# A Mamba-2 and attention trunk on one core: three steps of the gated norm moved one step ahead, a token half in a tile of its own, low parts set off the 256-byte line

## The chip, the cores and the metric

One core of one Trainium2 chip. The metric is the device time of one execution in microseconds, the median of three runs. The profile is that of one execution, taken by the hardware profiler. PE is the matrix engine (PEld its weight loads), DVE the vector engine, ACT the scalar engine, POOL the one that also issues some DMAs, SP the one whose queue issues most of them.

## What is computed

256 tokens of width 2048 run through a Mamba-2 layer, a gated MLP with a short convolution, an attention layer (one block of 256 keys, so plain causal attention with a distance penalty) and a second MLP. After each of the four, the stream is normalised:

```
mix = mamba2_mixer(h, ...)                    # layer 0
h = layer_norm(ALPHA * h + mix, g, b)
h = layer_norm(ALPHA * h + conv_ffn(h, ...), g, b)
k_blk, v_blk, k_mean = shared_kv(h, w_kv)
mix = moba_cross_attention(h, ...)            # layer 1
h = layer_norm(ALPHA * h + mix, g, b)
h = layer_norm(ALPHA * h + conv_ffn(h, ...), g, b)
```

The end of the Mamba-2 mixer, which the change touches, is for each of 8 groups of 512 channels

```
y = y * silu(z)
yg = y * rsqrt(mean(square(y)) + eps) * norm_w
```

All inputs are float32.

## The kernel before

**High and low parts.** Every float32 operand of a large product is split into a high part (rounded to fp32r) and a low part (the rest), and a product is made of three: high by high, low by high, high by low. A weight step is 512 KB: `load` fetches it into `raw` through SP's queue, `split` (L184, L185) has ACT write the high part `hi` and DVE the low part `lo`, each [128, 2, 512]. Four of each are held, and `splits` runs up to four steps ahead of the products. Activations live in `hT`, `yT`, `aT`, `gT`, with high and low part side by side.

**Chunks and steps.** The weights are cut into chunks of 512 output columns, the chunks into 882 steps of one weight tile each, all in one list worked off in order by the loop at the end. There are three modes:

- W (`whole`, L244 and L246): the weights are stationary, the activations move. A step has eight 512-wide matmuls on high parts (high and low activations beside each other) and eight 256-wide ones on low parts. Odd steps take the low parts first, so that runs of sixteen of a kind stand end to end. 560 steps are of this mode.
- X (`half`, L207, L208, L212): the activations are stationary, the weights move, 512 columns wide, once for each half of the 256 tokens, six matmuls a half.
- H: the dt chunk, with the same code as W.

All tiles in SBUF that TensorE reads in these modes start at one residue modulo 512 bytes, as their sizes are whole multiples of it (`LINE` pads small ones to 256 bytes).

**What runs beside the products.** `at(i, f)` puts a function behind the products of step i; `amid`, `within` and `beyond` put it inside a step. The instructions go to each engine in the order in which they are written, and every engine works off its own queue in order. For group g of the Mamba layer, with s0 the first step of its x chunk, the z chunk starts at s0 + 8 and the next group's x chunk at s0 + 16. `y_off` and `y_diag` (PE, then DVE) stand at s0 + 18; then `z_gate` (DVE, L768) at s0 + 20, `z_square` (ACT, L771) at s0 + 21, `z_sum` (two DVE additions, L775 and L776) at s0 + 22, `z_rms` (PE, L781, with the matrix of means) at s0 + 23, and five more steps to s0 + 28. The convolution of the next group has its taps on ACT (L575) and DVE (L580) behind step s0 + 21, and the decays on ACT (`m_decay`, L691) behind s0 + 21 and s0 + 22. POOL issues the loads of `mA` and `eA` (L668, L697) behind s0 + 19.

**The four sums and their norms.** `chain` works on the four X chunks of an output projection (`chs`, 2048 columns). As a chunk ends, `add2` or `add` (L393 to L406) adds ALPHA times the residual `r`, which `fetch` has loaded, and takes statistics. Chunk 3 is worked in another order, to have half 0 of the tokens normalised while half 1 is still summed: it has a `tail` of 4 steps (8 in the last of the four sums, `LAST`), in which only half 0 is done step by step, and half 1 of these steps comes at the end, in two pieces of 256 columns. In the kernel before, half 1 of this chunk is summed in the two pieces of 256 columns (`ch.piece`) in all its steps, tail or not: `second` calls `half` twice. The pieces lie in two of the three `acc` pairs of PSUM, in the last sum in the two `tp` tiles. `turn_half` (L349 on PE, L353 on ACT, L354 on DVE) turns normalised tokens back into `hT`, through `tp` tiles. The last sum keeps gains and shifts in free `acc` pairs (`gb_psum`, L454).

Of the kernel before, what the change touches and what calls it, by code (L numbers as in the profile page):

```python
# [19 lines left out]
F32R = mybir.dt.float32r  # L20
AF = mybir.ActivationFunctionType
OP = mybir.AluOpType
AX = mybir.AxisListType

P = 128
D = 2048
S = 256
# [9 lines left out]
ALPHA = 4.0 ** 0.25  # L37
LN_EPS = 1e-5
RMS_EPS = 1e-5
NC = 512  # L40
HC = NC // 2
NEG = -1.0e30
LINE = 64
# [10 lines left out]
WARM0 = 18  # L54
HEAD, TAIL = 3, 4
LAST = 8
SPARE = 3


# [32 lines left out]
def yoco_kernel(ctx: ExitStack, tc: tile.TileContext, x, lmg, lmb, lfg, lfb, x_t, columns, w, out):  # L92
    nc = tc.nc
    base = ctx.enter_context(tc.tile_pool(name="base", bufs=1))
    wts = ctx.enter_context(tc.tile_pool(name="wts", bufs=LA + 1))
# [8 lines left out]
    def acc_pair():  # L104
        return psum.tile([P, 2, NC], F32, tag="acc", name="acc", bufs=3)

    def tp_tile():
        return psum.tile([P, NC], F32, tag="tp", name="tp", bufs=2)
# [16 lines left out]
    steps, plan = [], chunks()  # L125
# [47 lines left out]
    def split():  # L173
        i = pos["split"]
        pos["split"] += 1
        t = raw_t.pop(i)
        if i in spare:
            h, l = (bufs["h"][:, k:k + 2].rearrange("p k a t -> p k (a t)") for k in (spare[i], spare[i] + 2))
        else:
            h = wts.tile([P, 2, NC], F32R, tag="hi", name="hi")  # L180
            l = wts.tile([P, 2, NC], F32R, tag="lo", name="lo")
        for e in ((0,), (1,)) if i < 2 else ((0, 1),):
            sl = slice(e[0], e[-1] + 1)
            nc.scalar.copy(h[:, sl], t[:, sl])  # L184
            nc.vector.tensor_sub(l[:, sl], t[:, sl], h[:, sl].bitcast(F32))  # L185
        hi_t[i], lo_t[i] = h, l
        load()
# [9 lines left out]
    def half(i, t, piece=None):  # L197

        ch, s = steps[i]
        h, l = hi_t[i], lo_t[i]  # L200
        sl = slice(0, NC) if piece is None else slice(piece * HC, (piece + 1) * HC)
        a = ch.part[t] if piece is None else ch.piece[piece]
        ts = slice(t * P, (t + 1) * P)
        for kk in range(2):
            k = 2 * s + kk
            th = ch.x.hi(k)[:, ts]
            nc.tensor.matmul(a, th, h[:, kk, sl], start=k == 0, stop=False)  # L207
            nc.tensor.matmul(a, th, l[:, kk, sl], start=False, stop=False)  # L208
        run(inner, (i, t, piece))
        for kk in range(2):  # L210
            k = 2 * s + kk
            nc.tensor.matmul(a, ch.x.lo(k)[:, ts], h[:, kk, sl], start=False, stop=k == ch.nk - 1)  # L212
        run(outer, (i, t, piece))

    def second(i):

        if steps[i][0].tail:
            half(i, 1, 0)
            half(i, 1, 1)
        else:  # L220
            half(i, 1)

    def done(i):
        hi_t.pop(i), lo_t.pop(i)
# [1 line left out]
    def whole(i):  # L226
        ch, s = steps[i]
        h, l = hi_t[i], lo_t[i]
        nj = ch.nj
        h, l = (t.rearrange("p a (k n) -> p (a k) n", n=nj * P) for t in (h, l))  # L230
        k0, half = ch.place(s)
        banks = [p[:, j, :] for p in ch.part[half:] for j in range(2)]

        parts = (1, 0) if s % 2 and ch not in calm else (0, 1)
        order = [(p, kk, j) for p in parts for kk in range(ch.per) for j in range(nj)]
        for n, (p, kk, j) in enumerate(order):
            if n == len(order) * 3 // 8:
                run(mid, i)
                splits(i)
            k = k0 + kk  # L240
            begins, ends = k == 0 and p == parts[0], k == ch.nk - 1 and p == parts[1]
            js = slice(j * P, (j + 1) * P)
            if p == 0:
                nc.tensor.matmul(banks[j], h[:, kk, js], ch.x.both(k), start=begins, stop=ends, skip_group_check=True)  # L244
            else:
                nc.tensor.matmul(banks[j][:, :S], l[:, kk, js], ch.x.hi(k), start=begins, stop=ends,  # L246
                                 skip_group_check=True)

    def products(i):
        ch, s = steps[i]  # L250
        if ch.mode == "W":
            if s == 0:
                ch.part = []
            if s == 0 or (not ch.both and s == ch.n // 2):
                ch.part += [acc_pair() for _ in range(1 + ch.both)]
        elif s == 0:
            a = acc_pair()
            ch.part = [a[:, 0, :], a[:, 1, :]] if ch.mode == "X" else [a]
            if ch.tail:
                ch.part.pop()  # L260
                ch.piece = [tp_tile()[:, :HC] if ch.tail == LAST else acc_pair()[:, 0, :HC] for _ in range(2)]
        if ch.mode != "X":
            whole(i)
            return done(i)
        half(i, 0)
        if i >= ch.end - ch.tail:
            if i < ch.last:
                return splits(i)
            for q in range(2):
                for j in range(ch.end - ch.tail, ch.end):  # L270
                    half(j, 1, q)
                    if q:
                        done(j)
        elif s < ch.head - 1:
            if ch.tail:
                splits(i)
        elif s == ch.head - 1:
            for j in range(ch.first, i + 1):
                if j < i or ch.tail:
                    splits(i, 1)  # L280
                second(j)
                done(j)
            if not ch.tail:
                splits(i, 1)
        else:
            run(mid, i)
            splits(i)
            second(i)
            done(i)
# [3 lines left out]
    def run(d, i):  # L293
        for f, a in d.get(i, []):
            f(*a)

    def at(i, f, *a):
        post.setdefault(i, []).append((f, a))
# [4 lines left out]
    def amid(i, f, *a):  # L303
        mid.setdefault(i, []).append((f, a))
# [5 lines left out]
    def beyond(i, t, q, f, *a):  # L310

        outer.setdefault((i, t, q), []).append((f, a))
# [52 lines left out]
    class Norm:  # L365
# [24 lines left out]
        def add(self, c, h, q=None):  # L390
            r = self.r[c][:, h]
            if q is None:
                nc.vector.scalar_tensor_tensor(r, r, ALPHA, self.chs[c].part[h], op0=OP.mult, op1=OP.add)  # L393
            else:
                v = r[:, q * HC:(q + 1) * HC]
                nc.vector.scalar_tensor_tensor(v, v, ALPHA, self.chs[c].piece[q], op0=OP.mult, op1=OP.add)
            for w in (0, 1) if q is None else (q,):
                nc.vector.bn_stats(self.st[:, h, 2 * c + w, :], r[:, w * HC:(w + 1) * HC])

        def add2(self, c):  # L400
            for h in range(2):
# [87 lines left out]
    chA = summed("a")  # L489
    up1, down1 = ffn_chunks(LAST)  # L490
    n_steps = len(steps)
# [325 lines left out]
    for g in range(NG):  # L817
        s0 = chX[g].first
        at(s0 + 3, m_load, g)
        at(s0 + 3, m_into, g)  # L820
        at(s0 + 7, m_cb, g)
        at(s0 + 9, m_bc, g)
        at(s0 + 5, m_decay, g, 0)
        at(s0 + 6, m_decay, g, 1)
        at(s0 + 9, m_exp, g, 0)
        at(s0 + 10, m_exp, g, 1)
        at(s0 + 10, m_into_exp, g)
        conv4(chX[g], 4 * g, lambda g=g: x_new(g), 0).plan()
        at(s0 + 11, x_silu, g)
        at(s0 + 11, m_mask, g, 0)  # L830
        at(s0 + 12, m_mask, g, 1)
        at(s0 + 13, x_turn, g)
        at(s0 + 13, y_d, g)
        for b in range(2):
            at(chZ[g].ready(b), z_gather, g, b)
            at(chZ[g].ready(b) + 1, z_silu, g, b)
        at(s0 + 18, y_off, g)
        at(s0 + 18, y_diag, g)
        at(s0 + 20, z_gate, g)
        at(s0 + 21, z_square, g)  # L840
        at(s0 + 22, z_sum, g)
        at(s0 + 23, z_rms, g)
        at(s0 + 24, z_log, g)
        at(s0 + 25, z_root, g)
        at(s0 + 26, z_newton, g)
        at(s0 + 27, z_scale, g)
        at(s0 + 28, z_split, g)


    def chain(norm, nxt=None, after=None):  # L850

        chs = norm.chs
        last = chs[3].last
        at(chs[0].first, norm.open)
        for c in range(4):
            at(max(chs[0].first, chs[c].last - 7), norm.fetch, c)
            if c < 3:
                at(chs[2].first + 3 + c, norm.fetch_gb, c)
                amid(chs[c].end, norm.add2, c) if c < 2 else beyond(chs[2].end, 0, None, norm.add2, c)
        beyond(last, 0, None, norm.add, 3, 0)  # L860
        beyond(last, 0, None, norm.stats, 0)
        if not nxt:
# [5 lines left out]
        n = nxt.first  # L868
# [49 lines left out]
    n3 = Norm(down1, keep(2), lfg[1], lfb[1], gb_last, lambda c: tok_view(out[0], c))  # L918
# [142 lines left out]
    for h in range(HEADS):  # L1061
        i, j = divmod(h, 4)
# [16 lines left out]
    end = n_steps - 1  # L1079
    chain(n3)  # L1080
    for e in range(4):
        spare[end - 3 + e] = 4 * e
    for c in (0, 2):
        at(down1[3].first + 6, n3.gb_psum, c)
    at(end - 6, n3.fetch_gb, 3)

    def rest(h):
# [62 lines left out]
```

## Time and profile before

| | |
|---|---|
| median of three runs | 2557.95 us (2557.05 to 2558.04) |
| span of the profiled execution, first to last instruction | 2555.2 us |
| granted TensorE clock, mean | 0.999 |
| HBM read | 492.30 MB, 196 GB/s |

The time of the profiled execution outside its span is not shown; the timed runs are 1.9 to 2.8 us longer than the span. In a row of the timeline the columns are start and length in microseconds, the engine, the line of the kernel, the operation, the output and the inputs by the program's names, the form, the count of instructions merged into the row, and in brackets how long the engine had been idle and what it waited for. Lengths of matmuls overlap, since they are pipelined; the distance of two starts is what one of them costs PE. A row of the groups has the summed busy time, the mean length of one in nanoseconds, and the idle time before. In the chain, pieces follow each other, each with its start and its share of the time.

### The profile page before, as it was taken

What the parts mean: (1) busy time and instruction counts of PE and PEld (TensorE: products, weight loads), DVE (VectorE), ACT (ScalarE), POOL (GpSimd) and SP (SyncE); (2) the same over time, 40 slices, a digit from 0 to 9 for tenths busy, and PEclk for the clock granted to TensorE, in tenths of its full rate; (3) what the DMA queues carried; (4) which work ended last, traced back from release to release, by engine and by line L of the source; (5) the groups of instructions that cost most, each with busy time, mean ns of one, the idle gap of its engine ahead of it and who ended that gap; (6) DMA issues with size and microseconds to landing.
All of it is one profiled execution on the core that took longest, in us unless ns stands there. A gap on an engine that the chain in (4) does not pass through costs nothing.

```text
span 2555.2 us, 36109 instructions
## 1 busy us (share of the span) xinstructions
PE 2532.8 (99%) x13999; PEld 2198.0 (86%) x13999; DVE 1660.4 (65%) x2130; ACT 1366.1 (53%) x1779; POOL 75.7 (3%) x96
## 2 busy tenths in 40 slices
PE   9999999999999999999999999999999999999998
PEld 8888888888888888888888888888888888888887
DVE  6878777864676667666444745655777676765545
ACT  6677677743465555555334444543555555554333
POOL 0000000000200000000000200000200000000001
PEclk9999999999999999999999999999999999999999
DMA  7655665557565565665666655456665655566564
GB/s 260 205 187 185 199 193 185 185 198 233 185 225 191 189 190 184 195 190 189 201 227 201 220 191 172 157 173 228 217 198 188 191 186 193 182 196 200 198 223 164
DMA packets 142266, 503.10 MB, mean 197 GB/s; under 512 B 15872, under 2 KB 16384, under 8 KB 142096
## 3 DMA queue, kind: packets, MB, share of 16 engines
q1 hardware_dynamic: 136976, 483.45, 57.8%
q0 software_dynamic: 4832, 16.85, 2.1%
q8 instruction: 109, 1.79, 0.3%
q14 instruction: 61, 0.50, 0.1%
q10 hardware_dynamic: 288, 0.52, 0.1%
HBM read 492.30 MB, written 8.45 MB: 196 GB/s over the span
## 4 chain that ended last, share of the span: by engine, by line
PE 94%; DVE 3%; ACT 1%; issue 1%; DMA 1%; SPq 0%; ACTq 0%; DVEq 0%
PE acc L244 38%; PE acc L246 20%; PE acc L212 11%; PE acc L208 11%; PE acc L207 11%; DVE lo L185 1%; DVE xc L580 1%; PE acc L743 1%; DMA raw<-in_w 1%; PE tp L212 0%; PE tp L208 0%; PE tp L207 0%; ACT hi L184 0%; PE tp L752 0%; PE acc L726 0%
## 5 line engine op out<-in xcount | busy, mean ns | idle before, releaser
L185 DVE TENSOR_TENSOR lo<-raw,hi 128x1024 fp32r<-128x1024 f32 (+1 forms) x871 | 1064.0, 1226 | 737.1 <-ACT hi L184 733.0
L184 ACT CAST hi<-raw 128x1024 fp32r<-128x1024 f32 (+1 forms) x871 | 911.3, 1048 | 909.6 <-PE acc L212 371.8
L244 PE MATMUL acc<-hT,hi 128*128 128x512 f32 x4496 | 1083.4, 392 | 0.7 <-ACT hi L184 0.7
L244 PEld LDWEIGHTS acc<-hT,hi 128*128 128x128 f32 x4496 | 824.6, 188 | 160.1 <-ACT hi L184 1.4
L246 PEld LDWEIGHTS acc<-hT,lo 128*128 128x128 f32 x4496 | 577.6, 191 | 23.9 <-issue 1.2
L246 PE MATMUL acc<-hT,lo 128*128 128x256 f32 x4496 | 587.4, 283 | 0.1
L208 PE MATMUL acc<-lo,gT 128*128 128x512 f32 (+1 forms) x678 | 254.5, 378 | 0.0
L207 PE MATMUL acc<-hi,gT 128*128 128x512 f32 (+1 forms) x678 | 254.1, 377 | 0.0
L212 PE MATMUL acc<-hi,gT 128*128 128x512 f32 (+1 forms) x678 | 200.8, 377 | 0.0
L208 PEld LDWEIGHTS acc<-lo,gT 128*128 128x128 f32 x678 | 127.6, 188 | 23.2
L207 PEld LDWEIGHTS acc<-hi,gT 128*128 128x128 f32 x678 | 127.6, 188 | 23.1
L212 PEld LDWEIGHTS acc<-hi,gT 128*128 128x128 f32 x678 | 124.9, 188 | 23.8
L207 PE MATMUL acc<-hi,yT 128*128 128x512 f32 (+1 forms) x270 | 98.7, 370 | 0.0
L208 PE MATMUL acc<-lo,yT 128*128 128x512 f32 (+1 forms) x270 | 98.6, 369 | 0.0
L207 PE MATMUL acc<-hi,hT 128*128 128x512 f32 x192 | 78.7, 410 | 0.0
L212 PE MATMUL acc<-hi,yT 128*128 128x512 f32 (+1 forms) x270 | 77.7, 369 | 0.0
L553 DVE TENSOR_TENSOR u<-u,acc 128x512 f32<-128x512 f32 x108 | 73.4, 680 | 5.9 <-ACT u L552 5.9
L580 DVE SCALAR_TENSOR_TENSOR g<-u,cols,g 128x254 f32<-128x254 f32 (+1 forms) x176 | 73.5, 478 | 4.9 <-ACT g L575 4.8
L208 PE MATMUL acc<-lo,hT 128*128 128x512 f32 x192 | 75.4, 393 | 0.0
L580 DVE SCALAR_TENSOR_TENSOR v<-u,cols,v 128x254 f32<-128x254 f32 (+1 forms) x176 | 73.1, 477 | 0.0
L965 ACT CAST gT<-v 128x512 fp32r<-128x512 f32 x44 | 27.3, 621 | 84.8 <-DVE v L964 84.8
L411 POOL TENSOR_TENSOR rs<-rs,mhalf 128x1 f32<-128x1 f32 x8 | 7.4, 931 | 2006.1 <-DVE nb L412 2006.1
(209 smaller groups left out, 1891.7 us busy)
## 6 DMA issues: line engine op xcount, KB each, us to landing
raw<-in_w SPq DMA_DIRECT2D x881, 512.0 KB, 4.1
mA<-acum_d POOLq DMA_DIRECT2D x16, 512.0 KB, 6.1
hres<-r POOLq DMA_DIRECT2D x12, 512.0 KB, 6.6
r<-hres SPq DMA_DIRECT2D x12, 512.0 KB, 4.5
eA<-acum_d POOLq DMA_DIRECT2D x16, 128.0 KB, 7.0
r<-in_x SPq DMA_DIRECT2D x4, 512.0 KB, 4.9
gb<-in_ln_mix_g SPq DMA_DIRECT2D x8, 256.0 KB, 5.6
gb<-in_ln_mix_b SPq DMA_DIRECT2D x8, 256.0 KB, 5.6
```

The source lines that it names most:

```text
L184: nc.scalar.copy(h[:, sl], t[:, sl])
L185: nc.vector.tensor_sub(l[:, sl], t[:, sl], h[:, sl].bitcast(F32))
L207: nc.tensor.matmul(a, th, h[:, kk, sl], start=k == 0, stop=False)
L208: nc.tensor.matmul(a, th, l[:, kk, sl], start=False, stop=False)
L212: nc.tensor.matmul(a, ch.x.lo(k)[:, ts], h[:, kk, sl], start=False, stop=k == ch.nk - 1)
L244: nc.tensor.matmul(banks[j], h[:, kk, js], ch.x.both(k), start=begins, stop=ends, skip_group_check=True)
L246: nc.tensor.matmul(banks[j][:, :S], l[:, kk, js], ch.x.hi(k), start=begins, stop=ends, skip_group_check=True)
L411: nc.gpsimd.tensor_tensor(self.rs[:, h, :], self.rs[:, h, :], mhalf[:, 0, :], op=OP.pow)
L553: nc.vector.tensor_add(dst, dst, p[:, :, :S])
L580: nc.vector.scalar_tensor_tensor(d, u[:, i % 2, :S - k], c1(self.at_w, w[n - 1 - k] + self.ia + i), d, op0=OP.mult, op1=OP.add)
L743: nc.tensor.matmul(ps[64 * q:64 * q + 64, c, j * P:(j + 1) * P], G[g]["xdt"][:, c, h * 64:(h + 1) * 64], G[g]["A", c][:, h, :], start=True ...
L965: nc.scalar.copy(h, v[:, sl])
```

## The change

Four things are changed:

- `z_gate`, `z_square` and `z_sum` move from s0 + 20, 21 and 22 to s0 + 19, 20 and 21. The rest of the chain stays where it was.
- In chunk 3 of each sum, the steps before the tail sum half 1 by 512 columns into an `acc` pair of its own. At the tail's first step the two pieces begin anew, the first in an `acc` pair, the second in a `tp` tile (in the last sum both in `tp`). `begin` adds ALPHA times the residual and the part summed so far, and the pieces are then added to that. `fetch` of chunk 3 comes a step earlier, in the last sum five; `gb_psum` of chunk 2 of the last sum comes later.
- The `lo` tile grows by 512 bytes. In W steps its two runs of 512 columns begin at 192 and at 2368 bytes from the tile's start, that is 192 and 64 bytes off the 256-byte line, and the low products take tiles in pairs from one and the other run by turns. In X steps the low part lies on the line as before.
- The space kept for POOL's DMA descriptors goes from its default of 16384 to 4096 bytes a partition.

```diff
+OFF = 48, 592
+LOW = 2 * (NC + LINE)
...
-            l = wts.tile([P, 2, NC], F32R, tag="lo", name="lo")
+            l = wts.tile([P, LOW], F32R, tag="lo", name="lo")
+            if steps[i][0].mode == "X":
+                l = l[:, :2 * NC].rearrange("p (k n) -> p k n", k=2)
+            else:
+                v = l[:, OFF[0]:OFF[0] + NC]
+                l = bass.AP(tensor=v.tensor, offset=v.offset, ap=[v.ap[0], [OFF[1] - OFF[0], 2], [1, NC]])
...
+        cut_k = ch.nk - 2 * ch.tail
+        first = 0 if piece is None else cut_k
+        last = (cut_k if t and piece is None else ch.nk) - 1
...
-            nc.tensor.matmul(a, th, h[:, kk, sl], start=k == 0, stop=False)
+            nc.tensor.matmul(a, th, h[:, kk, sl], start=k == first, stop=False)
...
     def second(i):
 
-        if steps[i][0].tail:
-            half(i, 1, 0)
-            half(i, 1, 1)
-        else:
-            half(i, 1)
+        half(i, 1)
...
-        order = [(p, kk, j) for p in parts for kk in range(ch.per) for j in range(nj)]
+        both = [divmod(n + a * NC // P, nj) for m in range(0, NC // P, 2) for a in range(2) for n in (m, m + 1)]
+        tiles = [[divmod(n, nj) for n in range(2 * NC // P)], both]
+        order = [(p, kk, j) for p in parts for kk, j in tiles[p]]
...
-                nc.tensor.matmul(banks[j][:, :S], l[:, kk, js], ch.x.hi(k), start=begins, stop=ends,
+                nc.tensor.matmul(banks[j][:, :S], l[:, a, n * P:(n + 1) * P], ch.x.hi(k), start=begins, stop=ends,
...
-            a = acc_pair()
-            ch.part = [a[:, 0, :], a[:, 1, :]] if ch.mode == "X" else [a]
-            if ch.tail:
-                ch.part.pop()
-                ch.piece = [tp_tile()[:, :HC] if ch.tail == LAST else acc_pair()[:, 0, :HC] for _ in range(2)]
+            b = acc_pair()
+            a = acc_pair() if ch.tail else b
+            ch.part = [a[:, 0, :], b[:, 0 if ch.tail else 1, :]] if ch.mode == "X" else [a]
+        elif ch.tail and i == ch.end - ch.tail:
+            ch.piece = [tp_tile()[:, :HC] if q or ch.tail == LAST else acc_pair()[:, 0, :HC] for q in range(2)]
...
-                nc.vector.scalar_tensor_tensor(v, v, ALPHA, self.chs[c].piece[q], op0=OP.mult, op1=OP.add)
+                nc.vector.tensor_add(v, v, self.chs[c].piece[q])
...
+        def begin(self, c, h):
+
+            r = self.r[c][:, h]
+            nc.vector.scalar_tensor_tensor(r, r, ALPHA, self.chs[c].part[h], op0=OP.mult, op1=OP.add)
...
-        at(s0 + 20, z_gate, g)
-        at(s0 + 21, z_square, g)
-        at(s0 + 22, z_sum, g)
+        at(s0 + 19, z_gate, g)
+        at(s0 + 20, z_square, g)
+        at(s0 + 21, z_sum, g)
...
-            at(max(chs[0].first, chs[c].last - 7), norm.fetch, c)
+            at(max(chs[0].first, chs[c].last - (7 if c < 3 else chs[3].tail + 4)), norm.fetch, c)
...
+        at(chs[3].end - chs[3].tail, norm.begin, 3, 1)
...
-    nc = _bacc.Bacc("TRN2", target_bir_lowering=False, num_devices=1)
+    nc = _bacc.Bacc("TRN2", target_bir_lowering=False, num_devices=1, dynamic_dma_scratch_size=4096)
```

More of the change, by code (lines that the diff above doesn't have):

```diff
@@ L211, in half @@
             k = 2 * s + kk
-            nc.tensor.matmul(a, ch.x.lo(k)[:, ts], h[:, kk, sl], start=False, stop=k == ch.nk - 1)
+            nc.tensor.matmul(a, ch.x.lo(k)[:, ts], h[:, kk, sl], start=False, stop=k == last)
         run(outer, (i, t, piece))
     def second(i):
-        if steps[i][0].tail:
-            half(i, 1, 0)
-            half(i, 1, 1)
-        else:
-            half(i, 1)
+        half(i, 1)
     def done(i):
@@ L229, in whole @@
         nj = ch.nj
-        h, l = (t.rearrange("p a (k n) -> p (a k) n", n=nj * P) for t in (h, l))
+        h = h.rearrange("p a n -> p (a n)")
         k0, half = ch.place(s)
@@ L234, in whole @@
         parts = (1, 0) if s % 2 and ch not in calm else (0, 1)
-        order = [(p, kk, j) for p in parts for kk in range(ch.per) for j in range(nj)]
-        for n, (p, kk, j) in enumerate(order):
-            if n == len(order) * 3 // 8:
+        both = [divmod(n + a * NC // P, nj) for m in range(0, NC // P, 2) for a in range(2) for n in (m, m + 1)]
+        tiles = [[divmod(n, nj) for n in range(2 * NC // P)], both]
+        order = [(p, kk, j) for p in parts for kk, j in tiles[p]]
+        for at_n, (p, kk, j) in enumerate(order):
+            if at_n == len(order) * 3 // 8:
                 run(mid, i)
@@ L241, in whole @@
             begins, ends = k == 0 and p == parts[0], k == ch.nk - 1 and p == parts[1]
-            js = slice(j * P, (j + 1) * P)
+            a, n = divmod(kk * nj + j, NC // P)
             if p == 0:
-                nc.tensor.matmul(banks[j], h[:, kk, js], ch.x.both(k), start=begins, stop=ends, skip_group_check=True)
+                nc.tensor.matmul(banks[j], h[:, (kk * nj + j) * P:(kk * nj + j + 1) * P], ch.x.both(k), start=begins, stop=ends, skip_group_check=True)
             else:
-                nc.tensor.matmul(banks[j][:, :S], l[:, kk, js], ch.x.hi(k), start=begins, stop=ends,
+                nc.tensor.matmul(banks[j][:, :S], l[:, a, n * P:(n + 1) * P], ch.x.hi(k), start=begins, stop=ends,
                                  skip_group_check=True)
@@ L1082, in yoco_kernel @@
         spare[end - 3 + e] = 4 * e
-    for c in (0, 2):
-        at(down1[3].first + 6, n3.gb_psum, c)
+    at(down1[3].first + 6, n3.gb_psum, 0)
+    at(end - LAST + 2, n3.gb_psum, 2)
     at(end - 6, n3.fetch_gb, 3)
```

## The prediction

> **What bounds the kernel now.** I read the page first (busy shares, groups), then the waits of PE, then the timelines of PE, DVE and ACT around the one wait that PE has.
>
> ```profile
> span 2555.2 us, 36109 instructions
> ...
> PE 2532.8 (99%) x13999; PEld 2198.0 (86%) x13999; DVE 1660.4 (65%) x2130; ACT 1366.1 (53%) x1779; POOL 75.7 (3%) x96
> ...
> L244 PE MATMUL acc<-hT,hi 128*128 128x512 f32 x4496 | 1083.4, 392 | 0.7 <-ACT hi L184 0.7
> ```
>
> PE is busy for 2532.8 of 2555.2 us, DVE for 65% and ACT for 53%. So only two things can move the end: a matmul stream that needs less time, or a hole in it that closes. The largest group is the 4496 512-wide matmuls of the W chunks on the high parts; beside each goes a 256-wide one on a low part (L246). On its own PE loses 0.7 us there: the stream itself is the bound. The timed median, 2557.95, is 2.75 us above this span (launch and end lie outside it); I take the sum against the span and add the 2.75 back.
>
> The hole: PE's waits name one place of weight.
>
> ```profile
> PE tp L781 <- DVE sz L776: 9.2, 7, 1.3
> ```
>
> L781 is `z_rms`, and it waits for `z_sum` (L775, L776) in seven of eight groups. The PE timeline of one group shows what it costs:
>
> ```profile
> 217.38 3.82 PE L244 MATMUL acc<-hT,hi 128*128 128x512 f32 x16
> 221.04 2.08 PE L246 MATMUL acc<-hT,lo 128*128 128x256 f32 x16
> 222.95 2.00 PE L244 MATMUL acc<-hT,hi 128*128 128x512 f32 x8
> 226.26 0.67 PE L781 MATMUL tp<-sz,mean 128*128 128x256 f32 x2 [1.31 <-DVE sz L776]
> ```
>
> Sixteen 512-wide start in 221.04 - 217.38 = 3.66 us, 0.229 each; sixteen 256-wide in 222.95 - 221.04 = 1.91, 0.119 each. Eight from 222.95 are through their starts at 222.95 + 8 x 0.229 = 224.78, and L781 starts at 226.26. The bracket's 1.31 is less, since it counts from the last matmul's end and not from when the next could start. **1.48 us a group.**
>
> **The gate and the squares a step sooner.** Why `z_sum` is late stands on DVE, and on ACT before it:
>
> ```profile
> 212.03 1.22 DVE L185 TENSOR_TENSOR lo<-raw,hi 128x1024 fp32r<-128x1024 f32 x1
> 214.99 1.23 DVE L185 TENSOR_TENSOR lo<-raw,hi 128x1024 fp32r<-128x1024 f32 x1 [1.74 <-ACT hi L184]
> 216.13 1.22 DVE L768 TENSOR_TENSOR y<-y,sz 128x1024 f32<-128x1024 f32 x1
> 217.26 0.68 DVE L553 TENSOR_TENSOR u<-u,acc 128x512 f32<-128x512 f32 x1
> 217.86 1.22 DVE L185 TENSOR_TENSOR lo<-raw,hi 128x1024 fp32r<-128x1024 f32 x1
> 221.37 2.55 DVE L580 SCALAR_TENSOR_TENSOR xc<-u,cols,xc 128x255 f32<-128x255 f32 x6 [2.29 <-ACT xc L575]
> ...
> 224.98 0.68 DVE L775 TENSOR_TENSOR sz<-sz 128x512 f32<-128x512 f32 x1
> 225.69 0.42 DVE L776 TENSOR_TENSOR sz<-sz 128x256 f32<-128x256 f32 x1
> ```
> ```profile
> 217.44 1.06 ACT L771 ACTIVATE sz<-y 128x1024 f32<-128x1024 f32 x1 [0.72 <-DVE y L768]
> 218.40 2.44 ACT L691 ACTIVATE mA<-mA,aux 128x128 f32<-128x128 f32 x8
> 220.75 1.08 ACT L575 ACTIVATE xc<-u,cols 128x256 f32<-128x256 f32 x2
> ```
>
> The squares are done at 218.50, but `z_sum` stands in DVE's queue behind six convolution taps (L580), which wait 2.29 us for ACT, which first works off eight decays (L691). Three instructions' places move; none is added, and no DMA among them. The gate (L768, 1.22 us) goes behind the split of 212.03, into DVE's hole of 1.74 us, from 213.25 to 214.5. The square (L771, 1.06) then runs on ACT from about 215; it stays ahead of the decays, so that L575 comes no later than now. `z_sum` (0.68 + 0.42) is queued ahead of the taps and fits the hole of 2.29 us before them. It ends near 220.2, over 4 us before PE asks at 224.78. The wait goes whole: 7 x 1.48 = **10.4 us**.
>
> What is late next is the split for step 1 of the following x chunk:
>
> ```profile
> 249.87 3.48 DVE L185 TENSOR_TENSOR lo<-raw,hi 128x1024 fp32r<-128x1024 f32 x3
> ```
> ```profile
> 252.46 2.08 PE L246 MATMUL acc<-hT,lo 128*128 128x256 f32 x16
> ```
>
> The first of those three splits ends near 251.1; its step begins with the second eight of the sixteen, at 252.46 + 8 x 0.119 = 253.4. It has 2.3 us; PE arriving 1.48 sooner leaves 0.8, and DVE has 1.1 us (`z_sum`) less to do on the way. I count nothing back, narrowly.
>
> **The tail chunk.** In chunk 3 of each of the four sums, every step runs token half 1 as twelve 256-wide matmuls; now only the last 4 (8 in the last sum) do, the others run six 512-wide. Steps changed: 16 + 22 + 8 + 22 - (4 + 4 + 4 + 8) = 48.
>
> ```profile
> 640.10 0.39 PE L207 MATMUL acc<-hi,yT 128*128 128x512 f32 x1
> ...
> 642.82 0.28 PE L207 MATMUL acc<-hi,yT 128*128 128x256 f32 x1
> ...
> 648.51 0.40 PE L207 MATMUL acc<-hi,yT 128*128 128x512 f32 x1
> 648.75 0.40 PE L208 MATMUL acc<-lo,yT 128*128 128x512 f32 x1
> ...
> 649.90 0.28 PE L207 MATMUL acc<-hi,yT 128*128 128x256 f32 x1
> 650.01 0.28 PE L208 MATMUL acc<-lo,yT 128*128 128x256 f32 x1
> ...
> 654.15 0.40 PE L207 MATMUL acc<-hi,yT 128*128 128x512 f32 x1
> ```
>
> Twelve 512-wide, which is a step of an ordinary X chunk, start in 642.82 - 640.10 = 2.72 us. Two steps of six 512-wide and twelve 256-wide lie between the rows of 648.51 and 654.15: 2.82 each. 0.10 x 48 = **4.8 us**. The added `begin` (four in all, like L553 one pass over 128x512 out of PSUM, 0.68 us) runs on DVE mid-chunk, one step behind the sum it reads; queued behind it are only splits. The residual is fetched a step sooner (five in the last sum) on SP. The new wait is for `tp`, of which a piece now holds one of two:
>
> ```profile
> 685.78 0.42 DVE L396 SCALAR_TENSOR_TENSOR r<-r,acc 128x256 f32<-128x256 f32 x1
> ```
> ```profile
> 686.98 0.60 PE L349 MATMUL tp<-ident,r 128*128 128x128 f32 x4
> ```
>
> The piece is read by 686.20, the transposes that need its slot come at 686.98: 0.8 us of cover, so nothing; without it some tenths of a microsecond at three hand-overs.
>
> **The low parts off the line.** This term is open: no run of before has a stationary low part off its line. 560 steps x 8 = 4480 low matmuls are touched. What the rows show is that a matmul's time is not fixed by its width. 256-wide stands at 0.119 in long runs, but the first behind a 512-wide run takes 650.01 - 649.90 = 0.11. 512-wide takes 2.72 / 12 = 0.227 in long runs, and the first behind a 256-wide run 648.75 - 648.51 = 0.24. So what is read beside it, and when, matters. For 256 wide the settled value is the worst that I see, for 512 wide it is near the best: moving the low parts alone can more easily gain than lose. A floor for a weight load with its matmul, from the chain's pieces in order of time:
>
> ```profile
> 244.34 0.87 PE acc L726 x8
> ```
>
> 0.109 each. Bounds: 4480 x (0.119 - 0.109) = 45 us gained; at the other end the 0.24 - 0.227 = 0.013 that an unsettled 512-wide one loses, 4480 x 0.013 = 58 us lost. I take halfway between 0.119 and the 0.11 of the nearest row (256 wide, fp32r, a load each), since the offset changes every second tile and the stream may settle again within a pair: 4480 x 0.0047 = **21 us**. DVE writes the same 128x1024 in two runs as before; I cost that at nothing.
>
> [...]
>
> **The smaller scratch** (POOL's DMA descriptors):
>
> ```profile
> mA<-acum_d POOLq DMA_DIRECT2D x16, 512.0 KB, 6.1
> ```
> ```profile
> 210.51 1.78 POOL L668 DMA_DIRECT2D mA<-acum_d  x2 [48.06 <-DVE y L756]
> ```
>
> Were one transfer allowed at a time, the first mA would land at 216.6 and the second at 222.7, and the decays on them (L691) start at 218.40 and one step later. Nothing, then.
>
> **Sum:** 10.4 + 4.8 + 21 = 36.2; 2555.2 - 36.2 + 2.75 = **2522**.
>
> **Rivals.** (1) *The offsets do nothing* (the change's last clause doesn't do what it is for): 2557.95 - 15.2 = 2543. For: no row tests an address. Against: the uneven times. (2) *The wait comes back*: the split's 0.8 us are used up once the low matmuls are quicker too, and PE waits for `lo` in place of `sz`; at worst 10.4 back: 2532. (3) *The other side:* the shifted reads fall in with the moving stream and every low matmul gets slower. It decides from 15.2 / 4480 = 3.4 ns a matmul upward, where it eats the other two terms; at the 13 ns above it gives 2557.95 - 15.2 + 58 = 2601, at half of that 2572. For: 512-wide do lose this. Against: no 256-wide one in these rows is above 0.12.
>
> **How the numbers follow.** Forecast 0.62; rival 1 0.20; rival 2 0.08; rival 3 0.10, of which 0.02 end within 0.2% (about 5 us, what a measurement can tell from no change). Faster 0.90, same 0.02, slower 0.08. The range goes from the full 45 us (2557.95 - 15.2 - 45 = 2498) to rival 1 with 3 us of the 15.2 missing (2546); beyond it lie rival 3 and less than 0.1 on the low side.
>
> **What would show it.** After: no wait of PE at L781, with L775 before L580 on DVE; no 256-wide rows in chunk 3 before its last steps; sixteen L246 in about 1.84 us instead of 1.91, with L244 unmoved at 3.66. Wrong if L246 keeps 1.91 (rival 1), exceeds 1.96 (rival 3), or if PE's waits list `lo` L185 with several us (rival 2); or if L244 changes too, which this sum leaves out.

## The result

| | before | after |
|---|---|---|
| median | 2557.73 us (2557.05 to 2558.04, 4 runs) | **2518.38 us** (2517.63 to 2519.19, 4 runs) |
| span of the profiled execution | 2555.2 us | 2516.6 us |
| granted TensorE clock, mean | 0.999 | 0.999 |

The ratio is 0.9847, with a 95% interval from 0.9833 to 0.9861. The change takes 39 us off; forecast were 36.2. Of the 39, 38.6 lie in the span; the profiled run of after is 1.95 us longer than its span, where the sum added 2.75. In the page of after, from the span, the busy shares and the groups:

```profile
span 2516.6 us, 35530 instructions
...
PE 2502.3 (99%) x13711; PEld 2159.3 (86%) x13711; DVE 1664.1 (66%) x2134; ACT 1366.1 (54%) x1779; POOL 75.8 (3%) x96
...
L252 PE MATMUL acc<-hT,hi 128*128 128x512 f32 x4496 | 1083.8, 392 | 0.5 <-ACT hi L191 0.5
...
L254 PE MATMUL acc<-hT,lo 128*128 128x256 f32 x4496 | 563.3, 277 | 0.9 <-DVE lo L192 0.9
```

In the page of before, the low group is

```profile
L246 PE MATMUL acc<-hT,lo 128*128 128x256 f32 x4496 | 587.4, 283 | 0.1
```

PE is still the bound, at 99% of a shorter span, and the 512-wide group (L252, which was L244) has kept its busy time: 1083.8 against 1083.4 us. The low group (L254, which was L246) has lost 24 us of its own. All the waits that PE has left, with the sum, the count and the longest:

```profile
PE tp L538 <- POOL ident masks.py:199: 1.4, 1, 1.4
PE acc L254 <- DVE lo L192: 0.9, 1, 0.9
PE acc L222 <- DVE hT L362: 0.6, 3, 0.2
PE acc L252 <- ACT hi L191: 0.5, 1, 0.5
PE tp L1063 <- DVE aT L1067: 0.3, 1, 0.3
PE tp L357 <- issue: 0.2, 1, 0.2
```

The row of 9.2 us is gone: `z_rms` (now L794) isn't in the list. Nothing of that size stands in its place. The `lo` wait of which rival 2 spoke is there once, with 0.9 us, and the transposes of the hand-over (L357, before L349) don't wait for DVE's read of the piece. The same group as in the prediction, in PE's timeline:

```profile
212.27 1.99 PE L254 MATMUL acc<-hT,lo 128*128 128x256 f32 x16
214.09 3.81 PE L252 MATMUL acc<-hT,hi 128*128 128x512 f32 x16
217.75 1.99 PE L254 MATMUL acc<-hT,lo 128*128 128x256 f32 x16
219.57 2.01 PE L252 MATMUL acc<-hT,hi 128*128 128x512 f32 x8
221.41 0.60 PE L794 MATMUL tp<-sz,mean 128*128 128x256 f32 x2
```

Sixteen 256-wide take 219.57 - 217.75 = 1.82 us, where they took 1.91; sixteen 512-wide take 217.75 - 214.09 = 3.66, as before. The last row has no bracket: L794 starts 1.84 us, eight 512-wide starts, behind the row above it. And DVE's timeline:

```profile
208.83 1.22 DVE L192 TENSOR_TENSOR lo<-raw,hi 128x1024 fp32r<-128x1024 f32 x1
209.97 1.22 DVE L781 TENSOR_TENSOR y<-y,sz 128x1024 f32<-128x1024 f32 x1
...
215.31 0.68 DVE L788 TENSOR_TENSOR sz<-sz 128x512 f32<-128x512 f32 x1
216.03 0.42 DVE L789 TENSOR_TENSOR sz<-sz 128x256 f32<-128x256 f32 x1
217.01 2.55 DVE L593 SCALAR_TENSOR_TENSOR xc<-u,cols,xc 128x255 f32<-128x255 f32 x6 [0.55 <-ACT xc L588]
```

`z_sum` (L788, L789) now stands ahead of the taps (L593) and ends at 216.45, 5 us before PE asks at 221.41.

The tail, in PE's timeline of chunk 3 of the first sum, where a step is now twelve 512-wide matmuls (before, it was six of them and twelve 256-wide ones):

```profile
636.17 0.39 PE L217 MATMUL acc<-hi,yT 128*128 128x512 f32 x1
...
638.89 0.39 PE L217 MATMUL acc<-hi,yT 128*128 128x512 f32 x1
...
662.01 0.28 PE L217 MATMUL acc<-hi,yT 128*128 128x256 f32 x1
```

A step takes 638.89 - 636.17 = 2.72 us instead of 2.82, and the first 256-wide one comes at 662.01, when only half 1 of the tail's 4 steps is left.

Where the time went, by the distances of starts of all matmuls of one form in the two traces:

| | before | after | difference |
|---|---|---|---|
| 256-wide on low parts of W and H, 4496 | 539.5 us (120.0 ns each) | 516.0 us (114.8 ns each) | -23.5 us |
| 512-wide on high parts, with what PE waits behind them | 1042.2 us | 1032.2 us | -10.0 us |
| the X chunks | 886.7 us | 882.3 us | -4.4 us |

These are 37.9 of the 38.6 us by which the two spans differ.

### The profile page after: what moved, and what is told of

Same layout as the page of the kernel before. It is cut to its first block, busy times and chain, and to the rows that moved or that the text cites. A ratio compares the mean times of both kernels' runs of the same rounds, so it can differ in the third digit from the quotient of the medians.

```text
span 2516.6 us, 35530 instructions
## 1 busy us (share of the span) xinstructions
PE 2502.3 (99%) x13711; PEld 2159.3 (86%) x13711; DVE 1664.1 (66%) x2134; ACT 1366.1 (54%) x1779; POOL 75.8 (3%) x96
## 2 busy tenths in 40 slices
DMA packets 142264, 503.07 MB, mean 200 GB/s; under 512 B 15872, under 2 KB 16384, under 8 KB 142096
## 4 chain that ended last, share of the span: by engine, by line
PE 96%; DVE 2%; DMA 1%; ACT 1%; issue 1%; SPq 0%; DVEq 0%; ACTq 0%
PE acc L252 40%; PE acc L254 20%; PE acc L222 11%; PE acc L217 11%; PE acc L218 11%; DVE lo L192 1%; DMA raw<-in_w 1%; PE acc L756 1%; ACT hi L191 0%; PE tp L765 0%; PE acc L739 0%; PE tp L1029 0%; DVE r L431 0%; PE tp L1063 0%; PE tp L217 0%
## 5 line engine op out<-in xcount | busy, mean ns | idle before, releaser
L252 PE MATMUL acc<-hT,hi 128*128 128x512 f32 x4496 | 1083.8, 392 | 0.5 <-ACT hi L191 0.5
L252 PEld LDWEIGHTS acc<-hT,hi 128*128 128x128 f32 x4496 | 822.3, 188 | 160.0 <-ACT hi L191 1.0
L254 PEld LDWEIGHTS acc<-hT,lo 128*128 128x128 f32 x4496 | 556.1, 188 | 24.7 <-DVE lo L192 1.3
L254 PE MATMUL acc<-hT,lo 128*128 128x256 f32 x4496 | 563.3, 277 | 0.9 <-DVE lo L192 0.9
L218 PE MATMUL acc<-lo,gT 128*128 128x512 f32 x668 | 259.6, 389 | 0.0
L217 PE MATMUL acc<-hi,gT 128*128 128x512 f32 x668 | 259.6, 389 | 0.0
L222 PE MATMUL acc<-hi,gT 128*128 128x512 f32 x668 | 205.5, 389 | 0.0
L217 PE MATMUL acc<-hi,yT 128*128 128x512 f32 x244 | 95.0, 389 | 0.0
L218 PE MATMUL acc<-lo,yT 128*128 128x512 f32 x244 | 94.7, 388 | 0.0
L593 DVE SCALAR_TENSOR_TENSOR g<-u,cols,g 128x254 f32<-128x254 f32 (+1 forms) x176 | 73.5, 478 | 4.8 <-ACT g L588 4.8
L222 PE MATMUL acc<-hi,yT 128*128 128x512 f32 x244 | 74.9, 388 | 0.0
L593 DVE SCALAR_TENSOR_TENSOR v<-u,cols,v 128x254 f32<-128x254 f32 (+1 forms) x176 | 73.1, 477 | 0.0
```

The costliest lines, as they stand in the source:

```text
L217: nc.tensor.matmul(a, th, h[:, kk, sl], start=k == first, stop=False)
L252: nc.tensor.matmul(banks[j], h[:, (kk * nj + j) * P:(kk * nj + j + 1) * P], ch.x.both(k), start=begins, stop=ends, skip_group_check=True)
L254: nc.tensor.matmul(banks[j][:, :S], l[:, a, n * P:(n + 1) * P], ch.x.hi(k), start=begins, stop=ends, skip_group_check=True)
L593: nc.vector.scalar_tensor_tensor(d, u[:, i % 2, :S - k], c1(self.at_w, w[n - 1 - k] + self.ia + i), d, op0=OP.mult, op1=OP.add)
```

## The experiments

**Each part alone.** Three kernels make one part of the change each, from the kernel before, timed beside it on one chip (before there: 2557.49, 13 runs). The intervals of the ratios are some 2.5 to 4 us wide to either side, so differences of 1 us between these kernels can't be told.

The gate alone:

```diff
-        at(s0 + 20, z_gate, g)
-        at(s0 + 21, z_square, g)
-        at(s0 + 22, z_sum, g)
+        at(s0 + 19, z_gate, g)
+        at(s0 + 20, z_square, g)
+        at(s0 + 21, z_sum, g)
```

> The kernel before with only z_gate, z_square and z_sum a step sooner. Theory (the three parts add up, each on its own stretch of PE): the wait of PE at z_rms goes in all seven groups, 7 x 1.48 = 10.4 us, so 2547.3 us, with no wait of PE at z_rms. Rival (the wait only moves): DVE's splits come late in its place and PE waits at the low matmuls for lo, with 2552 us or more.

Measured: 2547.02 us (2546.72 to 2547.56), ratio 0.9957 [0.9942, 0.9972], 10.5 us less. The largest rows of PE's waits:

```profile
PE tp L525 <- POOL ident masks.py:199: 1.4, 1, 1.4
PE acc L244 <- ACT hi L184: 1.1, 2, 0.5
```

L781 is gone and no wait for `lo` has come. The wait's row said 9.2, the distance of starts 10.4, and 10.5 came back: a bracket that counts from the last matmul's modelled end understates what a hole costs, here by 1.2 us over the seven.

The tail alone, that is the parts of the diff in `half`, `second`, the opening of the accumulators, `begin`, `fetch` and `gb_psum`:

```diff
+        first = 0 if piece is None else cut_k
+        last = (cut_k if t and piece is None else ch.nk) - 1
...
-            half(i, 1, 0)
-            half(i, 1, 1)
+        half(i, 1)
...
+        at(chs[3].end - chs[3].tail, norm.begin, 3, 1)
```

> The kernel before with only the tail chunk's change: half 1 by 512 columns before the tail, begin, the pieces begun anew. Theory: 48 steps x 0.10 us = 4.8 us, so 2552.9 us. Rival (the hand-over to the next stage pays, since a piece holds one of the two tp tiles): 2555 us or more, with PE's waits listing the transposes.

Measured: 2552.51 us (2552.05 to 2553.61, 10 runs), ratio 0.998 [0.9971, 0.999], 5.0 us less. PE's wait for `z_sum` (L785 here) has its old size, so the two parts don't touch each other:

```profile
PE tp L785 <- DVE sz L780: 9.2, 7, 1.3
```

The low parts alone, with the pair order, the longer tile and the smaller scratch:

```diff
+OFF = 48, 592
+LOW = 2 * (NC + LINE)
...
+        both = [divmod(n + a * NC // P, nj) for m in range(0, NC // P, 2) for a in range(2) for n in (m, m + 1)]
...
+    nc = _bacc.Bacc("TRN2", target_bir_lowering=False, num_devices=1, dynamic_dma_scratch_size=4096)
```

> The kernel before with only the low parts off the line, the low products by pairs of tiles, and the smaller scratch. Theory: every 256-wide low matmul goes from 0.119 to 0.114 us or a little less, 4480 x 0.005 = 23 us, so about 2534 us, and the wait at z_rms stays at 1.3 us a group in the list of PE's waits. Rival (quicker matmuls are eaten by waits for DVE and ACT, which have a sixth less room in the Mamba groups): 2540 us or more, and the wait at z_rms grows.

Measured: 2534.91 us (2533.55 to 2535.14), ratio 0.9908 [0.9891, 0.9924], 22.6 us less. In its waits and in its groups (low matmuls on L255):

```profile
PE tp L790 <- DVE sz L785: 10.5, 7, 1.5
PE acc L255 <- DVE lo L192: 0.8, 1, 0.8
```
```profile
L255 PE MATMUL acc<-hT,lo 128*128 128x256 f32 x4496 | 563.3, 277 | 0.9 <-DVE lo L192 0.8
```

The group has exactly the busy time of after. The wait for `z_sum`, still in this kernel, grew from 9.2 to 10.5: PE comes sooner and waits longer, which takes back 1.3 us of some 23.9. The three parts add up to 10.5 + 5.0 + 22.6 = 38.1 of the 39.1 us (2557.49 - 2518.38); this 1.3 would account for the missing 1.0, which is within the noise of the runs.

**Is it the offsets?** The low parts' edit is also another order of the tiles, a longer tile and a smaller scratch. This kernel is after with both offsets taken back to the line and all else kept:

```diff
-OFF = 48, 592
+OFF = 0, 576
```

> The changed kernel with both runs of the low part back on the 256-byte line (offsets 0 and 2304 bytes), the order by pairs of tiles and all else kept. Theory (the address of the weights modulo 256 decides): sixteen low matmuls take 1.91 us again, 0.119 each, and the time is 2518.4 + 23.5 = 2542 us. Rival (the order by pairs decides, or that two runs of the low part lie apart): sixteen stay at 1.82 us, and the time at 2518 us.

Measured: 2542.06 us (2541.83 to 2542.78), ratio 0.9938 [0.9923, 0.9953]. Before less the gate and the tail, as measured alone, is 2557.49 - 10.47 - 4.98 = 2542.04. So the order, the tile's length and the scratch are together worth nothing that these runs can tell (that the two agree to 0.02 us is chance), and the two offsets alone 2542.06 - 2518.38 = 23.7 us. In the group of low matmuls and in PE's timeline:

```profile
L254 PE MATMUL acc<-hT,lo 128*128 128x256 f32 x4496 | 587.1, 283 | 0.0
```
```profile
908.19 2.08 PE L254 MATMUL acc<-hT,lo 128*128 128x256 f32 x16
910.11 3.82 PE L252 MATMUL acc<-hT,hi 128*128 128x512 f32 x16
913.76 2.08 PE L254 MATMUL acc<-hT,lo 128*128 128x256 f32 x16
```

Sixteen 256-wide take 910.11 - 908.19 = 1.92 us again, and the 512-wide behind them 3.65. The busy time of the group differs by only 587.1 - 563.3 = 23.8 us, in agreement with the runs.

**Which offset?** The scans from here on are after with other offsets, changing from step to step, so that one kernel holds many cases; each was timed once, and what counts are distances of starts within it. "The line" is where the other tiles that these matmuls read begin, modulo 256 bytes. First one offset for both runs of a tile, in the plain order of tiles, from 0 to 240 bytes:

```diff
+                c = nth(i) // 2 % 16
+                off = 4 * c, 4 * c + NC + LINE
...
+        tiles = [[divmod(n, nj) for n in range(2 * NC // P)]] * 2
```

> The changed kernel with low products in the plain order of tiles and both runs of the low part at one offset, which goes through 0, 16, 32 to 240 bytes, a new one with each pair of W steps; so each run of sixteen low matmuls in the timeline has one offset. Theory (the weights' read and the moving read meet in the same stretch of a 256-byte period): the sixteen take 1.91 us at 0 and less at some others, changing with the offset in steps of 64 bytes, and best at 64 or 192 bytes, near 1.82. Rival (any offset off the 256-byte line does): 1.91 at 0 alone and about 1.82 at all the others. Second rival (only the change from one offset to the next helps): about 1.91 at all sixteen.

Measured: 2539.07 us (before beside it 2557.75), which with the gate and the tail in it is only some 3 us below the kernel on the line. The time of one low matmul by offset, the median of 17 or 18 runs of sixteen each:

```
bytes   0     16    32    48    64    80    96    112
ns    119.5 118.4 118.3 118.4 117.9 118.5 117.4 119.8
bytes 128    144   160   176   192   208   224   240
ns    120.3 119.0 120.1 117.9 117.8 116.6 116.6 117.1
```

PE's timeline where the offset is 0, and where it is 192 (L259 low, L257 high):

```profile
874.46 2.08 PE L259 MATMUL acc<-hT,lo 128*128 128x256 f32 x16
876.37 2.91 PE L257 MATMUL acc<-hT,hi 128*128 128x512 f32 x12
...
941.19 2.05 PE L259 MATMUL acc<-hT,lo 128*128 128x256 f32 x16
943.08 3.85 PE L257 MATMUL acc<-hT,hi 128*128 128x512 f32 x16
```

1.91 and 1.89 us; the best in the list, 116.6 ns, makes 1.87. In the median no single offset comes near the 1.82 of after, so that 64 or 192 does it by itself, as expected, isn't borne out. But at 64 bytes one run of the eighteen does:

```profile
1620.95 1.98 PE L259 MATMUL acc<-hT,lo 128*128 128x256 f32 x16
1622.77 2.01 PE L257 MATMUL acc<-hT,hi 128*128 128x512 f32 x8
```

1.82 us, with 113 or 114 ns for each of the sixteen, where the other seventeen have 117.9 in the mean. The next scan has (64, 64) among its cases, and there, too, one run of eighteen, at 127.04 us, has 113.4, and seventeen have 117.9. In these two runs the last 512-wide matmul ahead took 232 and 231 ns, in the other 34 between 225 and 229. So at one and the same offset the stream can settle in two ways, and how it comes in goes with which; no run was made to test that.

**The two together?** After's pair order, and all sixteen combinations of 0, 64, 128 and 192 bytes for the first and the second run:

```diff
+                c = nth(i) // 2 % 16
+                off = 16 * (c // 4), 16 * (c % 4) + NC + LINE
```

> The changed kernel, order by pairs kept, the two runs at all sixteen combinations of 0, 64, 128 and 192 bytes, a new one with each pair of W steps. Theory (each matmul's time follows from its own weights' offset): the time of sixteen is the mean of what the two offsets give alone, and two offsets alike do as well as two unlike ones. Rival (the change of offset every second tile is what helps): combinations of unlike offsets are quicker than both of their parts.

Measured: 2536.96 us. One combination stands out, first run 192 and second 64, with 113.8 ns a matmul; turned round, (64, 192) has 115.1, slower in its first eight and the same behind; the other fourteen lie between 117.8 and 120.3. In PE's timeline, (192, 64), (192, 128) and (192, 192) in a row (L259 low):

```profile
857.26 1.99 PE L259 MATMUL acc<-hT,lo 128*128 128x256 f32 x16
859.08 3.81 PE L257 MATMUL acc<-hT,hi 128*128 128x512 f32 x16
862.73 2.06 PE L259 MATMUL acc<-hT,lo 128*128 128x256 f32 x16
864.63 3.83 PE L257 MATMUL acc<-hT,hi 128*128 128x512 f32 x16
868.29 2.05 PE L259 MATMUL acc<-hT,lo 128*128 128x256 f32 x16
870.18 2.03 PE L257 MATMUL acc<-hT,hi 128*128 128x512 f32 x8
```

1.82, 1.90, 1.89. That a pair takes the mean of its two offsets' own times is refuted: 192 alone has 117.8 and 64 alone 117.9 (but for the two runs above), and in turns they have 113.8 in the median and 114.4 at most.

**Exactly these places?** Places near (192, 64), one or both moved, and the same two places 256 bytes further:

```diff
+PAIRS = ((192, 64), (448, 64), (192, 320), (64, 192), (208, 80), (176, 48), (224, 96), (160, 32), (192, 80), (192, 48), (208, 64), (176, 64), (192, 96), (192, 32), (224, 64), (160, 64))
...
+                o, r = (b // 4 for b in PAIRS[nth(i) // 2 % 16])
```

> The changed kernel with sixteen pairs of offsets for the two runs of the low part, a new one with each pair of W steps: 192 and 64; the same with 256 added to the one or to the other; 64 and 192; both shifted together by 16 or 32 bytes up and down; one of the two shifted by 16 or 32. Theory (the place modulo 256 decides, and the change by 128 bytes every second tile): 1.82 us for sixteen where 256 is added, and where both shift together it stays near 1.82; where one shifts alone it rises to 1.87 or more. Rival (the distance of the two runs in the tile decides, not their place modulo 256): adding 256 to one takes sixteen back to 1.88 or more.

Measured: 2531.59 us (before beside it 2557.45). (448, 64) and (192, 320) have the 113.8 of (192, 64): 256 bytes more on either run change nothing. Both moved together by 16 bytes have 117.7 and 118.0, by 32 bytes 119.4 and 118.1: the distance of the two places isn't enough, against the expectation. One of the two moved by 16 or 32 has 115.2 to 118.6. The first pair and the fifth in PE's timeline (L259 low):

```profile
871.75 1.98 PE L259 MATMUL acc<-hT,lo 128*128 128x256 f32 x16
873.58 3.81 PE L257 MATMUL acc<-hT,hi 128*128 128x512 f32 x16
...
893.67 2.04 PE L259 MATMUL acc<-hT,lo 128*128 128x256 f32 x16
895.55 2.68 PE L257 MATMUL acc<-hT,hi 128*128 128x512 f32 x11
```

(192, 64) has 1.83, (208, 80) 1.88.

**Must two tiles of one run follow each other?** The first half of the cases takes tiles from the two runs one and one, the second half four and four:

```diff
+        if nth(i) // 2 % 16 < 8:
+            both = [divmod(m + a * NC // P, nj) for m in range(NC // P) for a in range(2)]
+        else:
+            both = [divmod(n, nj) for n in range(2 * NC // P)]
```

> The changed kernel with other orders of the low tiles: one and one from the two runs by turns in half of the step pairs, four and four in the others, each with eight pairs of offsets (192 and 64, 64 and 192, 0 and 128, 128 and 0, 0 and 64, 64 and 0, 0 and 192, 192 and 0). Theory (two tiles that share their moving operand must share their offset, and the offset must change with the moving operand): no order of these reaches 1.82 us for sixteen; all lie between 1.85 and 1.93. Rival (a change of offset now and then is enough): 192 and 64 reach 1.82 in one of these orders too.

Measured: 2535.68 us. One and one, (64, 192) reaches 113.8, and (192, 64), whose first eight are slower, 116.7. Four and four, they have 116.7 and 117.5, but the last five of the sixteen of (64, 192) are at 113. The other places lie between 116.2 and 120.2 in either order. So the theory that two tiles of one place must follow each other falls; a change between 192 and 64 at every tile or at every second one brings the stream to 113 ns, and how soon differed with the order and with which of the two goes first.

**Against what is the place counted?** After, with 4160 bytes of scratch instead of 4096, which moves every tile in SBUF by 64 bytes and leaves all distances between tiles (in the programs as built, the tiles of these matmuls begin 128 bytes beyond a multiple of 256 in after, and 192 here):

```diff
-    nc = _bacc.Bacc("TRN2", target_bir_lowering=False, num_devices=1, dynamic_dma_scratch_size=4096)
+    nc = _bacc.Bacc("TRN2", target_bir_lowering=False, num_devices=1, dynamic_dma_scratch_size=4160)
```

> The changed kernel with 64 more bytes kept for POOL's descriptors, so that every tile in SBUF, weights, moving operands and low parts alike, lies 64 bytes further along; the distances between them stay. Theory (the distance of the weights from the moving operand modulo 256 decides): sixteen low matmuls stay at 1.82 us, and the time at 2518 us. Rival (the places themselves decide, that is on which 64 of 256 bytes the weights lie): sixteen go to 1.85 or more, and the time to 2525 us or more.

Measured: 2518.49 us (2516.91 to 2520.7, 4 runs), ratio 0.9848 [0.9831, 0.9864], no different from after. Its low group:

```profile
L254 PE MATMUL acc<-hT,lo 128*128 128x256 f32 x4496 | 563.4, 277 | 1.1 <-DVE lo L192 1.1
```

A move of 16 bytes of the weights alone loses most of the gain (117.7 and 118.0 ns against 113.8), and 64 bytes of everything lose nothing (563.4 us for the low group, 563.3 in after). So in these runs the place of the weights counts against the other tiles, of which the moving operand is the one that the same matmuls read.

**Can the 512-wide ones gain too?** No row had shown that there is something to gain. First the high parts with one offset from 0 to 240 bytes, changing with each run of sixteen:

```diff
+            h = wts.tile([P, LOW], F32R, tag="hi", name="hi")
...
+                c = (nth(i) + 1) // 2 % 16
+                v = h[:, 4 * c:4 * c + NC]
```

> The changed kernel with the high parts moved off the line too: offsets of 0, 16 to 240 bytes, a new one with each run of sixteen 512-wide matmuls. [...]

Measured: 2536.54 us. On the line a 512-wide matmul has 228.3 ns in the mean of a run, 240 bytes off 228.3, 192 off 228.7, 176 off 229.8, and all the rest 231.8 to 234.5. Offset 0 and then 16 in PE's timeline (L260 high):

```profile
869.86 3.81 PE L260 MATMUL acc<-hT,hi 128*128 128x512 f32 x16
873.51 1.99 PE L262 MATMUL acc<-hT,lo 128*128 128x256 f32 x16
875.33 3.90 PE L260 MATMUL acc<-hT,hi 128*128 128x512 f32 x16
879.06 1.99 PE L262 MATMUL acc<-hT,lo 128*128 128x256 f32 x16
```

3.65 and 3.73. Then the high parts in pairs of places, as with the low parts, and the weights of the X chunks, which move, at offsets from 0 to 240 bytes:

```diff
+                o = 4 * (nth(i, True) % 16)
...
+                offs = (16 * (c // 4), 16 * (c % 4) + NC + LINE), OFF
...
+        tiles = [both, both]
```

> The changed kernel with the high parts, too, taken by pairs of tiles from two runs, at all sixteen combinations of 0, 64, 128 and 192 bytes, a new one with each run of sixteen 512-wide matmuls; the low parts stay at 192 and 64. In X steps both parts, which move there, start 0, 16 to 240 bytes off the line, a new offset each step. Theory (an alternation of 192 and 64 settles each weights' read at a place where it costs 0.0067 us less, whatever the width): sixteen 512-wide at 192 and 64 take 16 x 0.0067 = 0.11 us less than 3.65, so 3.54. Rival (a 512-wide matmul is longer than the load beside it, so its start shifts against the next load in another way, and 192 and 64 are nothing special for it): no combination under 3.63. X steps: by theory and rival alike none quicker than 2.72 us at offset 0, since weights and activations there are settled on the line.

Measured: 2548.09 us (before beside it 2557.45), 30 us slower than after. High parts: (0, 0) is best with 228.3 ns, (192, 192) has 228.7, and (192, 64), the best of the low ones, 232.1. X chunks: 229.8 on the line, 227.3 at 240 bytes, 230 to 235 at the others, where they have 226.7 when all of them stay on the line. So no place that was tried does better for the 512-wide matmuls than the line when all stay on it, and for the 256-wide ones 192 and 64 by turns do best. No place in these scans brings sixteen 256-wide matmuls below 113.3 ns each, or the 512-wide ones below the 228.3 (stationary weights) and 226.7 (moving weights) of the line; for places that were not tried this says nothing.

## Why the prediction came out right

The forecast was 2522, the result 2518.4; each of its three terms was met within 3 us.

- **Gate, 10.4 forecast, 10.5 measured.** The mechanism was right down to the holes: the gate (209.97) stands right behind the split that was named for it (212.03 in before, 208.83 in after, where all of this comes some 3.2 us sooner), `z_sum` runs before the taps, and the wait goes whole. `z_sum` was to end 4.6 us before PE asks (220.2 and 224.78); it ends 5.0 us before (216.45 and 221.41).
- **What is late next, nothing forecast.** The split of the next x chunk was given 0.8 us to spare. After, in DVE's timeline:

```profile
245.52 3.49 DVE L192 TENSOR_TENSOR lo<-raw,hi 128x1024 fp32r<-128x1024 f32 x3
```

and in PE's:

```profile
247.21 1.99 PE L254 MATMUL acc<-hT,lo 128*128 128x256 f32 x16
```

The first of the three ends near 245.52 + 1.21 = 246.7, and the second eight begin at 247.21 + 8 x 0.114 = 248.1: 1.4 us to spare. DVE had moved up with PE, the split by 4.35 us and the matmuls by 5.25. Rival 2 would have needed several microseconds of `lo` waits; the list has 0.9.

- **Tail, 4.8 forecast, 5.0 measured alone**, and 4.4 by the starts in the X chunks of after. `begin` runs where it was put, and the `tp` piece is read without a wait behind it. In DVE's timeline:

```profile
661.09 0.68 DVE L411 SCALAR_TENSOR_TENSOR r<-r,acc 128x512 f32<-128x512 f32 x1
...
668.43 0.42 DVE L404 TENSOR_TENSOR r<-r,tp 128x256 f32<-128x256 f32 x1
```

- **Low parts, 21 forecast, 22.6 alone and 23.7 by the kernel on the line.** The sign and the size were right, and the 1.84 us for sixteen that was to show it came as 1.82. Forecast was 0.1145 us a matmul, halfway between 0.119 and 0.11; in after the first four behind a 512-wide run have 118, 116, 114 and 113 ns, and from there they have 113.3. That the size came out is luck, in two steps. The 0.11 is the difference of two rows of two decimals: in the trace's nanoseconds that matmul takes 113 (649.902 to 650.015), and the first low matmul behind a run of 512-wide ones in before takes 113.5 in the mean. Halfway between 119.5 and 113.5 the term would have been 4480 x 3 ns = 13 us, and the forecast near 2529. And the reason given for the halfway was wrong: the offset's change at every second tile was held against the term, as something that the stream has to settle from. In the scans it is with this change, between 192 and 64, that the stream settles, and it goes the whole way, from the 120 of before to 113.3, about what a first matmul took there; with one offset alone, by the medians, the term would have been at most 4480 x (119.5 - 116.6) ns = 13 us, and some 7 us at 64 or 192. So a sum that comes within 3 us rests here on a row whose cause was not known.
- **Rival 1** (the offsets do nothing, 2543, which is 2557.95 less the 10.4 + 4.8 = 15.2 us of gate and tail) is what the kernel with the offsets taken back gave, 2542.06: its price was right, its condition not met. **Rival 3** (the other side) has no place in these matmuls: at no offset did a run of 256-wide ones take more than 120.3 ns each. For the 512-wide ones, moved by themselves, it would have been true: 231.8 to 234.5 ns at twelve of the sixteen offsets, and 228.3 on the line. Its price was too high by the same two decimals: the 0.24 is 233 ns in the trace, so an unsettled 512-wide one loses 6 ns there, not 13.
- **Scratch: nothing**, as forecast, by the kernel on the line; nothing, too, for the order and the tile's length, which the sum left out.

What stays open is why these two places by turns lead to 113.3 ns in nearly every run, and 64 alone in two of 36. The runs show that 256 bytes more change nothing (113.8 ns), that the place of the weights counts against other tiles (16 bytes of the weights alone cost 4 ns, 64 bytes of everything nothing), and that place alone doesn't decide (113.4 and 117.9 ns at 64 bytes); which part of a matmul is slowed was not seen, and how two reads would meet is only inferred. The scratch was not run by itself either, but only with the other edits that came to nothing.

## What to carry to other kernels

Where PE is the bound at 99%, look at the distances of starts of its own matmuls: if one width has different times in different company, as 120 and 113 ns here, the operands' places in memory are worth a scan, which one run can hold by changing the place from step to step. Take such differences from more than two decimals, or from many matmuls at once. Take no single place from such a scan for the answer, since two places by turns did here what neither did reliably alone (113.8 ns against 117.8 and 117.9), and what helped one width hurt another (192 and 64 by turns gave a 512-wide matmul 232.1 ns in place of 228.3); and look at the single runs behind a median, since one place had two settled times here (113.4 and 117.9 ns at 64 bytes). And measure a hole in PE's stream by starts, not by the bracket of the wait, and look for its cause in the queue of the engine that PE waits for: seven waits went by moving three lines a step, with no work saved.

## What the runs showed of the hardware that was not expected

- A 256-wide fp32r matmul with a weight load of its own took 120.0 ns in long runs with weights and moving operand on one line, 113.3 ns with the weights 192 and 64 bytes off by turns, and 116.6 to 120.3, by the medians, with any one offset that was tried. At 64 bytes alone two runs of 36 had 113 to 114 throughout and the others 117.9, so the stream settled at two times at one and the same place.
- 256 bytes added to either place changed nothing (113.8 ns in all three cases), and both places moved by 16 bytes cost 4 ns (113.8 to 117.7 and 118.0) of the 5.7 gained.
- A 512-wide one did better at no place that was tried than with all of them on the line: 228.3 ns in the mean of a run against up to 234.5 with stationary weights off it, and 226.7 against up to 235 with moving weights off it.
- How soon the stream came to 113 ns differed with the order of the tiles and with which place went first: (192, 64) in pairs settled within four matmuls, (64, 192) only after six, and tile by tile (64, 192) settled within four and (192, 64) only after eleven.
